# Sending most of a result ahead of its last columns: one store, or two

## The chip, the cores and the metric

The kernel runs on one core of one Trainium2 chip. The metric is the device time of one execution in microseconds; quoted times are medians of several executions. All quoted runs are in the fast state with a granted clock of 1.0.

## The reference

```python
def setup_inputs():
    batch, seq, dim = 32, 512, 1024
    return {"x": np.random.randn(batch, seq, dim).astype(np.float32)}

def reference(x):
    relu_x = np.maximum(x, 0)
    return np.mean(relu_x, axis=-1).astype(np.float32)
```

It reads 67 MB and writes 64 KB: one mean for each of 16384 rows.

## The kernel before

The first 128 rows are handled on their own and stored early (512 bytes). The other 16256 are laid out as 128 partitions of 127 rows, so the results stand in a tile `res` of 128 x 127 floats. SyncE issues all loads on one queue: seven of 16 rows a partition, then pieces of 7, 4, 2 and 1 rows, then the last row of each partition in three pieces of columns. ScalarE and VectorE share the rows, and each writes a sum per row. GpSimd scales columns 0 to 111 once the seven big loads are reduced, columns 112 to 124 later, column 125 later still; VectorE writes column 126 itself, last of all. The cut below is the code of `before`, with comments added and lines left out at each `...`.

```python
    J = J - 1                       # 127 result columns
    NB = 16
    full = J // NB                  # 7 big loads
    j0 = full * NB                  # 112
    ...
    def finish(after, lo, hi):
        nc.gpsimd.wait_ge(act, after)
        nc.gpsimd.wait_ge(dve, after)
        nc.gpsimd.tensor_scalar(
            out=res[:, lo:hi], in0=sums[:, lo:hi], scalar1=inv, scalar2=0.0, op0=ALU.mult, op1=ALU.add,
        )
    ...
    finish(full, 0, j0)
    ...
    finish(i, j0, j0 + lo)
    ...
    nc.vector.wait_ge(loaded[i + 2], 16)                       # the middle column piece
    dve_row(nc, last[:, 512:768], last[:, D + 1:D + 2]).then_inc(dve, 1)
    nc.vector.wait_ge(act, n_done + 1)
    nc.vector.wait_ge(dve, n_done + 1)
    nc.vector.wait_ge(loaded[i + 3], 16)                       # the last column piece
    nc.vector.scalar_tensor_tensor(
        out=last[:, 768:], in0=last[:, 768:], scalar=0.0, in1=scale[:, :], op0=ALU.max, op1=ALU.mult,
        accum_out=res[:, J - 1:J],
    ).then_inc(dve, 1)

    nc.sync.wait_ge(pool, 2)
    nc.sync.wait_ge(dve, n_done + 2)
    nc.sync.dma_start(out=outr, in_=res[:, :]).then_inc(stored, 16)
    nc.sync.sem_clear(...)
    nc.sync.wait_ge(stored, 32).then_inc(stored, -32)
```

## Time and profile before

| | |
|---|---|
| time, median of 3 runs | 161.32 us (161.29 to 161.35) |
| span of the profile | 160.2 us |
| last load packet ends | 157.38 us |
| VectorE's last signal | 158.51 us |
| last landing of the store | 160.21 us |

The last three rows are from the trace's records of packets and of semaphore signals. The trace has 16 closing packets of 4 bytes and 16 semaphore signals for each load and store of the last stretch; a "landing" is such a signal, and the waiting engine goes on after the last of the 16. In this document the *tail* is the time from VectorE's last signal to the end of the span, 1.74 us here. Only the tail is the store's; what comes before it is the stream of loads and the last reductions.

### The profile page before, as it was taken

Reading aid. Unit: us, or ns where it says so; the run is one execution under the profiler, and the core shown is the slowest. Engines: PE = TensorE matmul, PEld = TensorE weight load, DVE = VectorE, ACT = ScalarE, POOL = GpSimd, SP = SyncE. Lnnn points to the kernel's source line nnn. Section 1 sums busy time; section 2 is a strip of 40 time slices with the busy share of each in tenths; the row PEclk is TensorE's granted clock in tenths of the full one; section 3 lists DMA queues with packets and bytes.
Section 4 is the critical chain, followed back from the end, with each engine's and each line's share of the span. In section 5 each row is a group of like instructions: output and inputs, shape, how many; then the busy total and the mean of one; then the engine's idle time right before and its main releaser. Section 6 shows DMA issues by size and latency. Waiting matters only on the chain. (4 is left out here: it accounts for less than half of the span.)

```text
span 160.2 us, 347 instructions
## 1 busy us (share of the span) xinstructions
DVE 73.3 (46%) x131; ACT 70.4 (44%) x133; POOL 1.3 (1%) x9
## 2 busy tenths in 40 slices
DVE  0000029900498006960079500993009920299984
ACT  1400029800496006950079300991009900299983
POOL 1000000000000000000000000000000000000001
DMA  9969969979989899699699699699699797998992
GB/s 393 507 278 523 507 278 523 442 344 523 409 376 523 360 425 524 294 491 523 262 524 523 262 523 524 262 523 523 262 524 458 327 523 327 425 451 367 419 412 102
DMA packets 2312, 67.18 MB, mean 419 GB/s; under 512 B 392, under 2 KB 648, under 8 KB 1032
## 3 DMA queue, kind: packets, MB, share of 16 engines
q1 hardware_dynamic: 2312, 67.18, 97.7%
HBM read 67.11 MB, written 0.07 MB: 419 GB/s over the span
## 5 line engine op out<-in xcount | busy, mean ns | idle before, releaser
L20 DVE TENSOR_SCALAR_CACHE_REDUCE rows<-rows 128x1024 f32<-128x1024 f32 (+1 forms) x63 | 72.1, 1208 | 78.9 <-DMA rows<-in_x_dram 78.7
L15 ACT ACTIVATE rows<-rows 128x1024 f32<-128x1024 f32 x64 | 66.2, 1035 | 84.1 <-DMA rows<-in_x_dram 83.9
L15 ACT ACTIVATION_READ_ACCUMULATOR rows<-rows 128x1 f32 x64 | 11.9, 186 | 0.0
L20 DVE DVE_READ_ACCUMULATOR rows<-rows 128x1 f32 x63 | 5.2, 82 | 0.0
L168 DVE STREAM_TRANSPOSE turned<-mean 128x32 f32<-128x32 f32 x1 | 0.2, 213 | 5.9 <-ACT row L164 5.9
L164 ACT ACT_TABLE_LOAD x1 | 1.3, 1283 | 3.3 <-DMA row<-in_x_dram 3.3
L157 POOL TENSOR_SCALAR res<-sums 128x112 f32<-128x112 f32 (+1 forms) x2 | 0.5, 250 | 154.0 <-DVE rows L20 154.0
L164 ACT ACTIVATE row<-row 128x1024 f32<-128x1024 f32 x1 | 1.1, 1056 | 0.0
L15 ACT ACTIVATE last<-last 128x512 f32<-128x512 f32 x1 | 0.6, 630 | 0.0
L20 DVE TENSOR_SCALAR_CACHE_REDUCE last<-last 128x256 f32<-128x256 f32 x1 | 0.4, 420 | 0.3 <-DMA last<-in_x_dram 0.3
L197 DVE SCALAR_TENSOR_TENSOR last<-last,scale 128x258 f32<-128x258 f32 x1 | 0.4, 428 | 0.1
L142 POOL MEMSET scale<- 128x258 f32 x1 | 0.3, 314 | 0.0
L187 POOL TENSOR_SCALAR res<-part 128x1 f32<-128x1 f32 x1 | 0.3, 267 | 0.6 <-DVE rows L20 0.6
L164 ACT ACTIVATION_READ_ACCUMULATOR row<-row 128x1 f32 x1 | 0.2, 186 | 0.0
L15 ACT ACTIVATION_READ_ACCUMULATOR last<-last 128x1 f32 x1 | 0.2, 186 | 0.0
L141 POOL MEMSET mean<- 128x32 f32 x1 | 0.1, 126 | 1.5 <-POOLq L55 1.5
L232 POOL MEMSET const-uint8-127<- 128x1 uint8 x1 | 0.1, 103 | 0.0
L232 POOL MEMSET const-bfloat16-1.0<- 128x1 bf16 x1 | 0.1, 102 | 0.0
L232 POOL MEMSET const-float32-0.0<- 128x1 f32 x1 | 0.1, 99 | 0.2 <-issue 0.2
L232 POOL MEMSET const-float32-1.0<- 128x1 f32 x1 | 0.1, 99 | 0.0
L20 DVE DVE_READ_ACCUMULATOR last<-last 128x1 f32 x1 | 0.1, 83 | 0.0
L197 DVE DVE_READ_ACCUMULATOR last<-last,scale 128x1 f32 x1 | 0.1, 82 | 0.0
## 6 DMA issues: line engine op xcount, KB each, us to landing
rows<-in_x_dram SPq DMA_DIRECT2D x1, 3584.0 KB, 38.1
rows<-in_x_dram SPq DMA_DIRECT2D x1, 2048.0 KB, 42.6
rows<-in_x_dram SPq DMA_DIRECT2D x1, 1024.0 KB, 44.7
row<-in_x_dram SPq DMA_DIRECT2D x1, 512.0 KB, 3.3
rows<-in_x_dram SPq DMA_DIRECT2D x1, 512.0 KB, 45.4
last<-in_x_dram SPq DMA_DIRECT2D x1, 256.0 KB, 45.6
last<-in_x_dram SPq DMA_DIRECT2D x2, 128.0 KB, 45.4
rows<-in_x_dram SPq DMA_DIRECT2D x7, 48.8
```

The source lines that it names most:

```text
L15: return nc.scalar.activation(out=src, in_=src, func=ACT.Relu, accum_out=acc)
L20: return nc.vector.tensor_scalar(out=src, in0=src, scalar1=0.0, scalar2=init, op0=ALU.max, op1=ALU.add, accum_out=acc,)
L141: nc.gpsimd.memset(mean0[:, :], 0.0)
L142: nc.gpsimd.memset(scale[:, :], inv).then_inc(pool, 1)
L157: nc.gpsimd.tensor_scalar(out=res[:, lo:hi], in0=sums[:, lo:hi], scalar1=inv, scalar2=0.0, op0=ALU.mult, op1=ALU.add,)
L164: nc.scalar.activation(out=row0[:, :], in_=row0[:, :], func=ACT.Relu, scale=inv, accum_out=mean0[:, 0:1],).then_inc(first, 1)
L168: nc.vector.transpose(turned0[:, :], mean0[:, :]).then_inc(first, 1)
L187: nc.gpsimd.tensor_scalar(out=res[:, J - 2:J - 1], in0=part[:, 0:1], scalar1=part[:, 1:2], scalar2=inv, op0=ALU.add, op1=ALU.mult,).then_i ...
L197: nc.vector.scalar_tensor_tensor(out=last[:, 768:], in0=last[:, 768:], scalar=0.0, in1=scale[:, :], op0=ALU.max, op1=ALU.mult, accum_out=r ...
L232: nc = _bacc.Bacc("TRN2", target_bir_lowering=False, num_devices=1)
```

## The change

The intent is to take bytes off the store that stands at the end: 112 of the 127 columns have been ready since about 149 us. They go out in a store of their own, queued behind the loads, and the last store carries 15 columns.

```diff
@@ in finish
             out=res[:, lo:hi], in0=sums[:, lo:hi], scalar1=inv, scalar2=0.0, op0=ALU.mult, op1=ALU.add,
-        )
+        ).then_inc(pool, 1)
@@ at the end
     nc.sync.wait_ge(pool, 2)
+    nc.sync.dma_start(out=outr[:, :j0], in_=res[:, :j0]).then_inc(stored, 16)
     nc.sync.wait_ge(dve, n_done + 2)
-    nc.sync.dma_start(out=outr, in_=res[:, :]).then_inc(stored, 16)
+    nc.sync.wait_ge(pool, 4)
+    nc.sync.dma_start(out=outr[:, j0:], in_=res[:, j0:]).then_inc(stored, 16)
 ...
-    nc.sync.wait_ge(stored, 32).then_inc(stored, -32)
+    nc.sync.wait_ge(stored, 48).then_inc(stored, -48)
```

## The prediction

> **What bounds the kernel now.** I read the page first, for the shares of busy time and the slices, then the waits, then the timeline of the last four microseconds, and last a table of short stretches at the end of the span with the packet records of the trace beside it.
>
> The page says what holds the kernel as a whole:
>
> ```profile
> span 160.2 us, 347 instructions
> DVE 73.3 (46%) x131; ACT 70.4 (44%) x133; POOL 1.3 (1%) x9
> ...
> q1 hardware_dynamic: 2312, 67.18, 97.7%
> HBM read 67.11 MB, written 0.07 MB: 419 GB/s over the span
> ```
>
> The two computing engines are busy less than half of the span, and the packets on the one DMA queue fill 97.7% of it. So the kernel is a stream of 67 MB of loads, with a short head and a short tail around it. The change touches no load; all it can move lies in the tail, between the last load packet (ends at 157.38 us in the packet records) and the end of the span at 160.24 us: 2.86 us, 1.8% of the span.
>
> The waits of the issuing queue say the same from its side (columns: total us, times, longest):
>
> ```profile
> SPq L204 <- DVE last L197: 45.6, 1, 45.6
> SPq L210 <- SPq L210: 1.2, 1, 1.2
> ```
>
> From the end of its last load issue (112.9 us) to the end of the last reduction at 158.5 us the queue does nothing: it waits 45.6 us for VectorE, issues the store, and then waits 1.2 us for the store to land. The page's chain of work that ended last gives 0% to everything: it stops at a branch hint in the tail, so I built the chain from the timeline instead (start, duration):
>
> ```profile
> 157.54 0.42 DVE L20 TENSOR_SCALAR_CACHE_REDUCE last<-last 128x256 f32<-128x256 f32 x1 [0.29 <-DMA last<-in_x_dram]
> 157.70 0.19 ACT L15 ACTIVATION_READ_ACCUMULATOR last<-last 128x1 f32 x1
> 157.89 0.08 DVE L20 DVE_READ_ACCUMULATOR last<-last 128x1 f32 x1
> 158.06 0.43 DVE L197 SCALAR_TENSOR_TENSOR last<-last,scale 128x258 f32<-128x258 f32 x1
> 158.41 0.08 DVE L197 DVE_READ_ACCUMULATOR last<-last,scale 128x1 f32 x1
> 158.57 0.35 SPq L205 DMA_DIRECT2D out_dram<-res  x1
> ```
>
> VectorE was released by the middle column piece at 157.54, ran the two last reductions to 158.49, and the store was issued at 158.57. The stretches from there on (length, busy times of DVE, ACT and POOL, clock, then the DMA share and GB/s):
>
> ```profile
> 158.49:158.57 0.08, 0.01 (x1) 0.00 (x0) 0.00 (x0) 1.00 0.00 0
> 158.57:159.41 0.84, 0.00 (x0) 0.00 (x0) 0.00 (x0) 1.00 0.00 0
> 159.41:159.78 0.37, 0.00 (x0) 0.00 (x0) 0.00 (x0) 1.00 0.61 176
> 159.78:160.24 0.46, 0.00 (x0) 0.00 (x0) 0.00 (x0) 1.00 0.00 0
> ```
>
> So the store's 1.67 us from issue to end are 0.84 us in which no packet moves, 0.37 us of packets, and 0.46 us from the last packet to the last landing. Only the middle one can depend on bytes by anything seen here.
>
> **What the Trainium skill says.** Three places of the page "DMA: Bandwidth & Descriptors" bear on it. The section "Anatomy of one DMA — SWDGE (gpsimd) path" gives a transfer a fixed part of about 2 us, mostly the receipt of the last write, and a part that grows with bytes. It describes another issuing path, but the trace has the same shape: of 1.67 us, 1.30 (0.84 + 0.46) move no data. The section "Queues, rings and completion order" says that on each DMA engine the descriptors of a ring are consumed in ring order; the trace agrees for the loads, whose 16 closing packets for each of the last three pieces come in order. The section "Rules for kernel authors" says of small transfers to coalesce them, since under 64 KB one pays mostly overhead: both parts of the divided store are such transfers (56 KB and 7.5 KB), so by that rule one store is better unless the first part's overhead is hidden. No page speaks of how two waits ahead of one transfer are placed; for that I use the trace.
>
> **The change part by part.**
>
> Removed: one store of 128 rows of 127 floats (508 bytes a row) at the end. In its place at the end is one of 128 rows of 15 floats (60 bytes a row), as many descriptors as before. The duration of one packet in the trace's records, by size: 4 bytes 9 ns, 128 bytes 13, 508 bytes 27, 1024 bytes 46, 2048 bytes 84. This is a line: (46 - 27) / (1024 - 508) = 0.037 ns a byte, and 27 - 508 x 0.037 = 8.2 ns fixed. A 60 byte packet is then an estimated 8.2 + 2.2 = 10.4 ns. Each of 16 engines moves 8 rows: 8 x 27 = 216 ns now, 8 x 10.4 = 83 after, 133 ns less. The engines start staggered: their closing packets start between 159.607 and 159.762, so less 216 ns their first data packets start about 159.39 to 159.55. If the stagger stays, the end moves by the full 0.13 us. If the descriptors are supplied no faster than they are consumed now, the end moves by less; I count 0.11 us. The 0.84 us and the 0.46 us stay.
>
> Added early: one store of 128 rows of 112 floats (448 bytes, an estimated 24.7 ns a packet, 8 x 24.7 = 0.2 us an engine). It waits for GpSimd's first scaling, which runs at 148.68 for 0.29 us, so it is issued at about 149.0 on a queue that otherwise sleeps until 158.5: its 0.35 us of issue cost nothing. Its packets lie behind the loads in the rings, start on each engine when that one's last load is done (closing packets between 156.99 and 157.37), and are over by about 157.6, or 158.1 with a landing of 0.46 us. The final packets do not start before 159.4, so the two stores do not meet, and the last wait (now for 48 instead of 32) is still ended by the second one.
>
> Moved: the waits. Now the store has two waits, written GpSimd first, VectorE second. The trace shows the second as an instruction of its own (the VectorE wait is counted at L204, and 17 ns long) and the first one carried by the transfer itself; the loads with two waits have the same split. From VectorE's signal at 158.507 to the issue at 158.57 are 0.063 us. In the change VectorE's wait is written first, so by the same rule the transfer itself carries it. Instructions that carry the wait that ends last start 17 to 24 ns after the signal in this tail (VectorE's at 157.542 after the landing at 157.518; the final wait at 160.226 after 160.209). So 0.04 us may be saved; since no transfer here shows it, I count 0.03. No instruction is added on the path.
>
> GpSimd's two added signals ride on existing instructions of an engine that is 1% busy: nothing.
>
> Sum: -0.11 - 0.03 = -0.14 us. 161.32 - 0.14 = 161.18 us, 0.09% less.
>
> **The rivals.**
>
> First, nothing moves at the end: the tail is latency and the number of descriptors, which is the same 128. Against it: in the 0.37 us of packets the mean DMA share is 0.61, and the engines' own packets lie one behind the other, so these are bytes being moved. For it: I have seen no 60-byte packet, and rows that start at odd multiples of 4 bytes may cost more on the memory side than the line says. The section "Specifications" of the same page says that below 512 bytes a transfer does read-modify-write; 508 and 60 are both below, and no run shows yet whether it is dearer for 60. Then 161.3.
>
> Second, the early store delays the last loads. Its packets begin on the first engine at 157.0, while the slowest engine still reads its last piece until 157.37. That last piece has landed at 157.82, and VectorE, with its own earlier work, goes on only at 157.98, so there are 0.16 us of slack for it. The middle piece has none (157.518 to 157.542), but its last closing packet started at 156.97, before any packet of the early store can start. So only a delay over 0.16 us would count; 8 packets of 25 ns on an engine that is already done with its loads can hardly make one. If they did, perhaps +0.1 to +0.2: 161.4.
>
> Third, the second transfer is slower to issue or land because the first was issued: it writes the rest of the same rows of memory. The first has landed more than a microsecond before. 161.4 at most.
>
> A fourth, the intent: that the store's whole cost hides behind the loads. It cannot: the last columns are known only at 158.49, and a transfer with 1.30 us of fixed time follows whatever its size. This would make it 159.7 only if the last store vanished.
>
> **Range and chances.** All the rivals lie within -0.3 and +0.25 us of 161.32. Three runs of before lie within 0.06 us, and a different instruction stream may shift a run by some 0.1. So 161.18 us, with 160.95 to 161.40 eight times in ten. Two per cent is 3.2 us, more than the whole tail of 2.86, so faster by over 2% is impossible but for a side effect on the loads, and slower by that much would need the loads disturbed for microseconds: 0.01 each, 0.98 within 2%.
>
> **What would show it.** Each step has its place in the profile of the changed kernel. The early store's issue stands at about 149.0. Its 128 packets of 448 bytes stand between 157.0 and 157.6, and VectorE's two last reductions still end near 158.5. The gap from the end of the last reduction to the store's issue shrinks from 0.08 to about 0.04. The stretch with packets of 60 bytes is about 0.24 us long instead of 0.37, and those ahead and behind stay at 0.84 and 0.46. It would be wrong if the packets of 60 bytes last nearer 27 ns than 10, if the stretch after the last packet grows, or if the last reductions start later than 158.06 because the last column piece lands later.

## The result, and the profile after

| | before | after |
|---|---|---|
| median of 6 runs each, same rounds | 161.40 us (161.29 to 161.78) | 161.19 us (161.07 to 161.81) |
| ratio | | 0.9989, 95% interval 0.9971 to 1.0008 |

A ratio is the mean time of one kernel's fast runs over the mean of the other's in the same rounds, so it is not quite the ratio of the medians. The clock alone cannot even tell the sign for sure, since single executions of one kernel differ by up to 0.7 us here. The trace can: from profile to profile the pieces of the tail that should not change differ by 23 ns at most (one landing of 444 ns, where the others are near 400, is looked into below).

The page of the changed kernel (the total, and the one queue: packets, MB, share):

```profile
span 159.8 us, 348 instructions
...
q1 hardware_dynamic: 2456, 67.18, 97.9%
```

One instruction more, the second transfer, and 144 packets more, its 128 rows and 16 closing packets. The bytes are the same.

The waits of the issuing queue after (total us, times, longest):

```profile
SPq L205 <- POOL res L157: 35.9, 1, 35.9
SPq L207 <- POOL res L187: 8.3, 1, 8.3
SPq L213 <- SPq L213: 1.0, 1, 1.0
SPq L208 <- DVE last L197: 0.7, 1, 0.7
```

The one wait of 45.6 us is now three: until GpSimd has scaled 112 columns, then until it has done the rest, then 0.7 us for VectorE. The final wait for the landing is 1.0 us instead of 1.2. Note that VectorE's wait is now counted at L208, the line of the transfer itself, where before it had a line of its own.

The timeline of the queue and of VectorE's last instructions after (start, duration):

```profile
148.81 0.35 SPq L205 DMA_DIRECT2D out_dram<-res  x1
...
157.84 0.43 DVE L197 SCALAR_TENSOR_TENSOR last<-last,scale 128x258 f32<-128x258 f32 x1
158.19 0.08 DVE L197 DVE_READ_ACCUMULATOR last<-last,scale 128x1 f32 x1
158.30 0.34 SPq L208 DMA_DIRECT2D out_dram<-res  x1
```

and the stretches of the tail after (length, busy times, clock, DMA share, GB/s):

```profile
158.27:158.30 0.03, 0.01 (x1) 0.00 (x0) 0.00 (x0) 1.00 0.00 0
158.30:159.14 0.84, 0.00 (x0) 0.00 (x0) 0.00 (x0) 1.00 0.00 0
159.14:159.36 0.22, 0.00 (x0) 0.00 (x0) 0.00 (x0) 1.00 0.42 35
159.36:159.78 0.42, 0.00 (x0) 0.00 (x0) 0.00 (x0) 1.00 0.00 0
```

Compared with the four stretches of before in the prediction: the stretch between the last reduction and the issue shrank from 0.08 to 0.03, the wait for the first packet stayed 0.84, the packets take 0.22 instead of 0.37, and the stretch after them is 0.42 instead of 0.46.

The span fell by 0.46 us, more than twice what the clock shows. Only 0.24 of it is the tail (1.736 to 1.496 us). The other 0.22 us was there before the tail began: the last load packet ended at 157.13 instead of 157.38. The packets of the second load, issued at 0.45 us in both, started at 2.52 instead of 2.75, so the stream had that difference from its start. Nothing of the change lies there, and the repeats below show that it is chance.

### The profile page after: what moved, and what is told of

Same layout as the page of the kernel before. It is cut to its first block, busy times and chain, and to the rows that moved or that the text cites. A ratio compares the mean times of both kernels' runs of the same rounds, so it can differ in the third digit from the quotient of the medians.

```text
span 159.8 us, 348 instructions
## 1 busy us (share of the span) xinstructions
DVE 73.3 (46%) x131; ACT 70.4 (44%) x133; POOL 1.3 (1%) x9
```

## The experiments

The theory: the change gains in two places of the tail and nowhere else. The last store's packets are shorter (60 bytes in place of 508), about 0.14 us, and the transfer itself now carries VectorE's wait, about 0.05 us. Rivals: the gain is one of these alone; it needs the large store to be hidden behind the loads; it is the 0.22 us by which the loads ended earlier; the larger landing (0.44 and 0.40) belongs to the kernel before.

This table, worked out from the packet and signal records of each profile, is what the experiments are read by. All in ns. "Gap" is from VectorE's last signal to the start of the issue that follows; "first" from that issue to the first packet of the last store; "packets" from the first packet's start to the last one's end, with the median of one packet in brackets; "landing" from there to the last landing. A further 33 or 34 to the end of the span complete the tail. (The kernel with two stores at the end doesn't fit the columns and is told below.)

| kernel | row bytes of the last store | gap | first | packets (one) | landing | tail |
|---|---|---|---|---|---|---|
| before | 508 | 63 | 848 | 347 (27) | 444 | 1736 |
| before, again | 508 | 63 | 843 | 354 (27) | 396 | 1690 |
| order of the waits only | 508 | 17 | 843 | 349 (27) | 391 | 1634 |
| after | 60 | 16 | 838 | 207 (11) | 402 | 1496 |
| after, again | 60 | 16 | 840 | 207 (11) | 402 | 1498 |
| after, old order of waits | 60 | 63 | 839 | 208 (11) | 393 | 1536 |
| large store late | 60 | 17 | 840 | 203 (11) | 397 | 1490 |
| cut in half | 252 | 16 | 844 | 260 (18) | 390 | 1543 |
| three stores | 8 | 17 | 827 | 193 (9) | 384 | 1454 |
| eight early stores | 60 | 17 | 829 | 203 (11) | 780 | 1863 |
| eight early stores, again | 60 | 17 | 825 | 207 (11) | 792 | 1875 |
| eight early stores by rows | 60 | 16 | 846 | 207 (11) | 400 | 1503 |
| small rows in one early store | 60 | 16 | 842 | 209 (11) | 1914 | 3014 |

The times of the experiments, in three groups that each shared a chip and its runs of before:

| kernel | median us | before, same rounds | ratio, 95% interval |
|---|---|---|---|
| order of the waits only | 161.41 | 161.37 | 1.0003 (0.9986 to 1.0020) |
| after, old order of waits | 161.18 | 161.37 | 0.9979 (0.9966 to 0.9993) |
| large store late | 161.12 | 161.37 | 0.9979 (0.9965 to 0.9993) |
| after, again | 161.13 | 161.37 | 0.9978 (0.9964 to 0.9993) |
| cut in half | 161.33 | 161.42 | 1.0000 (0.9984 to 1.0015) |
| eight early stores | 161.39 | 161.42 | 0.9990 (0.9978 to 1.0002) |
| two at the end | 161.76 | 161.42 | 1.0024 (1.0010 to 1.0039) |
| before, again | 161.34 | 161.42 | 0.9999 (0.9987 to 1.0012) |
| small rows in one early store | 163.13 | 161.39 | 1.0110 (1.0091 to 1.0128) |
| eight early stores by rows | 161.32 | 161.39 | 1.0000 (0.9981 to 1.0020) |
| three stores | 161.17 | 161.39 | 0.9988 (0.9969 to 1.0007) |
| eight early stores, again | 161.85 | 161.39 | 1.0022 (1.0009 to 1.0035) |

All results were correct but the one that is wrong.

### The order of the waits alone

The kernel before, with two lines changing places:

```diff
-    nc.sync.wait_ge(pool, 2)
     nc.sync.wait_ge(dve, n_done + 2)
+    nc.sync.wait_ge(pool, 2)
     nc.sync.dma_start(out=outr, in_=res[:, :]).then_inc(stored, 16)
```

> One store as in the kernel before; only its two waits change places, VectorE's first. Tail means the time from VectorE's last signal to the end of the span: 1.74 us in the profile of before, 1.50 in that of the change. Theory (two gains in the tail: the order of the waits, and the shorter packets): the gap from that signal to the store's issue falls from 0.063 to about 0.016 us, the packets stay 27 ns and last 0.35 us in all, the tail is 1.69, the time 0.05 us less than before (not to be told from it by the clock alone). Rival (the order of the waits has nothing to do with it, the short gap came from the wait for GpSimd that was over early): the gap stays 0.06.

The gap fell from 63 to 17 ns, and the packets stayed at 27 ns and 0.35 us. The stretches from the issue on:

```profile
158.24:159.09 0.85, 0.00 (x0) 0.00 (x0) 0.00 (x0) 1.00 0.00 1
159.09:159.44 0.35, 0.00 (x0) 0.00 (x0) 0.00 (x0) 1.00 0.64 185
159.44:159.86 0.42, 0.00 (x0) 0.00 (x0) 0.00 (x0) 1.00 0.00 0
```

The theory's gap is right. The tail is 1.63 and not the expected 1.69, because the landing took 391 ns instead of 444; that was not expected of this experiment. The clock shows no gain (161.41 against 161.37); one of 0.05 us is too small for it.

### The change with the old order of the waits

```diff
-    nc.sync.wait_ge(dve, n_done + 2)
     nc.sync.wait_ge(pool, 4)
+    nc.sync.wait_ge(dve, n_done + 2)
     nc.sync.dma_start(out=outr[:, j0:], in_=res[:, j0:]).then_inc(stored, 16)
```

> The change, but with the two waits of the last store in the old order (GpSimd's first). Theory: gap 0.063 us as before, packets of 60 bytes at 11 ns, 0.21 us in all, tail 1.50 + 0.05 = 1.55; time about 0.15 to 0.2 us under before. Rival (all of the gain is the waits): the packets are short but the tail is 1.7.

```profile
158.71:158.79 0.08, 0.00 (x1) 0.00 (x0) 0.00 (x0) 1.00 0.00 0
158.79:159.62 0.83, 0.00 (x0) 0.00 (x0) 0.00 (x0) 1.00 0.00 0
159.62:159.84 0.22, 0.00 (x0) 0.00 (x0) 0.00 (x0) 1.00 0.42 35
```

The gap is back at 63 ns and the packets are as short as in the change: 1.536 us of tail. With the run above, the two gains are separate and add up: 46 or 47 ns for the waits, 139 to 147 ns for the packets. This profile is of the longest of its five executions (161.60 us), in which the loads ended late, at 157.59; its tail was no longer for that.

### The large store issued late

```diff
-    nc.sync.wait_ge(pool, 2)
+    nc.sync.wait_ge(pool, 4)
     nc.sync.dma_start(out=outr[:, :j0], in_=res[:, :j0]).then_inc(stored, 16)
```

> The change, but the large store is issued only when GpSimd has done everything, at about 157.5 us instead of 148.8, so it is not queued behind the loads and moves at about 158.4, with the DMA engines idle before it. Theory (what counts is only that the bytes left the last store, wherever they went before it): the last store's issue, packets and landing as in the change, tail 1.50, time as the change's. Rival (the gain needs the large store hidden behind the loads): the last store's first packet or landing comes later, by up to 0.3 us, and the time is that of before or more.

```profile
157.47 0.35 SPq L205 DMA_DIRECT2D out_dram<-res  x1
...
158.26 0.34 SPq L208 DMA_DIRECT2D out_dram<-res  x1
```

```profile
158.31:158.66 0.35, 0.00 (x0) 0.00 (x0) 0.00 (x0) 1.00 0.59 164
158.66:159.10 0.44, 0.00 (x0) 0.00 (x0) 0.00 (x0) 1.00 0.00 0
159.10:159.32 0.22, 0.00 (x0) 0.00 (x0) 0.00 (x0) 1.00 0.42 35
159.32:159.73 0.41, 0.00 (x0) 0.00 (x0) 0.00 (x0) 1.00 0.00 0
```

The first stretch is now the large store, alone on the DMA engines and 0.44 us ahead of the small one. The tail is 1.490, that of the change, and so is the time. The place behind the loads is worth nothing by itself; it was enough that the large store was issued 0.78 us before VectorE's last signal (157.47 and 158.25). A later issue was not tried, but for both stores at the end, below.

### The change again, and the kernel before again

> The change once more, for a second profile. Theory: tail 1.50 within 0.05, wherever the loads end; the end of the load packets may move by 0.2 us either way between profiles. Rival (the difference of the two spans, 0.46 us, is all the work of the change): the load packets end at 157.13 again and the span is 159.8 again within 0.05.

> The kernel before once more, for a second profile. Theory: gap 0.063, packets of 27 ns in 0.35 us, and the landing after the last packet about 0.40, as in the four other new profiles, since the 0.444 of the first profile was chance: tail 1.69. Rival (the old kernel's landing is longer by 0.04 by its nature): 0.44 again, tail 1.74.

The second profile of the change has the same tail to 2 ns (1.498). Its span is 159.842, within the 0.05 us that the rival allowed, and its loads ended at 157.15, so this run alone does not refute that rival. The second profile of before does: its loads ended at 157.14, where they end in the changed kernel, and its span is 159.99 us, not 160.24.

```profile
158.29:158.36 0.07, 0.00 (x0) 0.00 (x0) 0.00 (x0) 1.00 0.00 0
158.36:159.20 0.84, 0.00 (x0) 0.00 (x0) 0.00 (x0) 1.00 0.00 0
159.20:159.57 0.37, 0.00 (x0) 0.00 (x0) 0.00 (x0) 1.00 0.61 176
159.57:159.98 0.41, 0.00 (x0) 0.00 (x0) 0.00 (x0) 1.00 0.00 0
```

So the first profile of before had a late stream of loads and a long landing (444 against 396), both by chance. (Its execution took 161.59 us, where the three timed runs took 161.29 to 161.35.) Between like profiles the change is worth 1.690 - 1.496 = 0.194 us.

### Another cut

```diff
-    nc.sync.dma_start(out=outr[:, :j0], in_=res[:, :j0]).then_inc(stored, 16)
+    nc.sync.dma_start(out=outr[:, :64], in_=res[:, :64]).then_inc(stored, 16)
 ...
-    nc.sync.dma_start(out=outr[:, j0:], in_=res[:, j0:]).then_inc(stored, 16)
+    nc.sync.dma_start(out=outr[:, 64:], in_=res[:, 64:]).then_inc(stored, 16)
```

> The change cut at another column: 64 columns go out early, the last 63 (252 bytes a row) at the end. Theory (the last store's packets cost 8.2 ns plus 0.037 ns a byte, eight to an engine one after the other): packets of 17.5 ns, the stretch of packets 0.347 - 8 x (27 - 17.5) / 1000 = 0.27 us, tail 1.49 + 0.06 = 1.55 to 1.56. Rival (a step, not a line: any row under some size is as cheap as 60 bytes, or any row is as dear as 508 but for very small ones): 11 ns and 0.21 us, or 27 ns and 0.35 us.

```profile
159.31:159.59 0.28, 0.00 (x0) 0.00 (x0) 0.00 (x0) 1.00 0.54 115
```

18 ns a packet, 0.26 us of packets, tail 1.543: the line holds at this size too, and neither step of the rival is there. The times, 161.33 against 161.42, are too close to add to that.

### Two stores at the end

```diff
-    nc.sync.wait_ge(pool, 2)
-    nc.sync.dma_start(out=outr[:, :j0], in_=res[:, :j0]).then_inc(stored, 16)
     nc.sync.wait_ge(dve, n_done + 2)
     nc.sync.wait_ge(pool, 4)
     nc.sync.dma_start(out=outr[:, j0:], in_=res[:, j0:]).then_inc(stored, 16)
+    nc.sync.dma_start(out=outr[:, :j0], in_=res[:, :j0]).then_inc(stored, 16)
```

> Both stores at the end, the 15 columns first and the 112 columns right behind them, none early. Theory (the fixed time of a store hides only where nothing waits for it; at the end each further transfer costs its issue): second issue some 0.39 us after the first and 0.44 long, first of its packets 0.5 us after that, packets 0.32, landing 0.40: tail 2.05 to 2.10, time 0.35 us over before. Rival (issuing is cheap beside moving, two transfers in a row overlap wholly): tail 1.65 to 1.75, time that of before.

```profile
158.34 0.35 SPq L206 DMA_DIRECT2D out_dram<-res  x1
158.73 0.43 SPq L207 DMA_DIRECT2D out_dram<-res  x1
```

The second issue starts 0.39 us after the first, its first packet comes at 159.66, and the tail is 2.09 us: a second transfer costs 0.4 us where something waits for it. The time is 0.34 us over before in the medians, and clear of it. The same two transfers are 0.19 us better or 0.4 us worse in the tail than one, by when the first of them is issued.

### Eight early stores

```diff
-    nc.sync.dma_start(out=outr[:, :j0], in_=res[:, :j0]).then_inc(stored, 16)
+    for k in range(0, j0, 14):
+        nc.sync.dma_start(out=outr[:, k:k + 14], in_=res[:, k:k + 14]).then_inc(stored, 16)
 ...
-    nc.sync.wait_ge(stored, 48).then_inc(stored, -48)
+    nc.sync.wait_ge(stored, 160).then_inc(stored, -160)
```

> The change, but the early 112 columns go out in eight stores of 14 columns instead of one, all queued behind the loads: 1024 packets of about 10 ns, some 0.7 us on each engine instead of 0.2, with eight times the closing packets. Theory (behind the loads in the rings they can't delay a load, and they are done before 159): the last column piece lands 0.44 to 0.49 us after the last load packet, as in all five profiles so far, VectorE's last signal comes 1.13 to 1.20 us after it, tail 1.50, time as the change's. Rival (stores on engines that are done with their loads slow the others' last piece or its landing): the landing takes 0.6 us or more, and the time rises by 0.15 us or more.

This went against the theory. The last packets of the early stores ended at 157.65, well before 159, but:

```profile
158.35:159.18 0.83, 0.00 (x0) 0.00 (x0) 0.00 (x0) 1.00 0.00 0
159.18:159.40 0.22, 0.00 (x0) 0.00 (x0) 0.00 (x0) 1.00 0.42 35
159.40:160.20 0.80, 0.00 (x0) 0.00 (x0) 0.00 (x0) 1.00 0.00 0
```

The last store's packets are unchanged and its landing takes twice as long, 780 ns, which neither the theory nor the rival had foreseen. The landing of the last column piece of the loads also rose, from 475 ns after the last load packet to 614, as the rival had it; VectorE's slack took that up (its last signal came 1.18 us after the last load packet, in the theory's range). The clock shows no loss against before (161.39 and 161.42). The run's six times fell between 161.08 and 161.54, and the profile is of one of the longest, so the experiment was repeated:

> The eight early stores of 14 columns once more, since its six runs fell into two groups (161.08 to 161.25 and 161.54) and its profile was of the slow group. If the long landing is there in every execution: last landing 0.6 to 0.8 again and a median near 161.4. If it is a chance of some executions: a profile with a landing of 0.40 goes with a time near 161.1.

The landing was 792 ns this time, and all six times lay between 161.63 and 162.02, with a median of 161.85 where 161.4 was expected. The loads' last landing came even later, 729 ns after the last load packet, and this was more than VectorE's slack: its last signal came 1.30 us after that packet. The two profiled executions differ by 0.47 us: the loads ended 0.34 us later, VectorE's signal came another 0.11 us later, and the tails differ by 0.01. The tail's loss is there in both profiles, but both are of longer executions of their runs (161.54 and 162.01), so it is not shown for those of 161.08 to 161.25. Why the six executions of the first run were on average 0.5 us faster is not explained.

### Which property of the eight stores does it

Two more kernels take apart what the eight stores have more of: small rows, and closing packets. The first is wrong (every 14th of the early columns isn't written), so as to have the small rows in a single transfer:

```diff
-    nc.sync.dma_start(out=outr[:, :j0], in_=res[:, :j0]).then_inc(stored, 16)
+    gaps = lambda ap: ap.rearrange("p (a b) -> p a b", b=14)[:, :, :13]
+    nc.sync.dma_start(out=gaps(outr[:, :j0]), in_=gaps(res[:, :j0])).then_inc(stored, 16)
```

> Wrong result on purpose: the early columns go out in one store again, but as eight pieces of 13 columns a row with one column left out after each, so 1024 packets of 52 bytes with only 16 closing packets (the eight-store run had 1024 packets of 56 bytes with 128 closing packets; its early landings trailed from 157.4 to 159.3 us, though its packets ended at 157.65, and its last landing took 0.78 us in place of 0.40). Theory A (many small writes to memory are received more slowly than their packets run): the same trail, early landings until 159, the last store's landing 0.6 to 0.8 us, tail 1.7 to 1.9. Theory B (it is the number of closing packets): early landings done by 158.3, last landing 0.40, tail 1.50.

The second has eight transfers with the change's 128 packets of 448 bytes:

```diff
-    nc.sync.dma_start(out=outr[:, :j0], in_=res[:, :j0]).then_inc(stored, 16)
+    for p in range(0, P, 16):
+        nc.sync.dma_start(out=outr[p:p + 16, :j0], in_=res[p:p + 16, :j0]).then_inc(stored, 16)
 ...
-    nc.sync.wait_ge(stored, 48).then_inc(stored, -48)
+    nc.sync.wait_ge(stored, 160).then_inc(stored, -160)
```

> Eight early stores again, but cut by rows: 16 rows of 112 columns each, so 128 packets of 448 bytes as in the change, with 128 closing packets in place of 16. Theory A (small writes): early landings done by 158.1, last landing 0.40, tail 1.50, as in the change. Theory B (closing packets): the trail and the long last landing as with eight stores of 14 columns, tail 1.7 to 1.9.

The last stretch of each, from the last packet to the end; first the small rows in one store, then the eight stores by rows:

```profile
159.73:161.66 1.93, 0.00 (x0) 0.00 (x0) 0.00 (x0) 1.00 0.00 0
```

```profile
159.52:159.94 0.42, 0.00 (x0) 0.00 (x0) 0.00 (x0) 1.00 0.00 0
```

The long last landing goes with the 1024 small rows and not with the closing packets: 1914 ns with 16 closing packets, 400 ns with 128. The eight stores by columns and those by rows show the same with 128 closing packets and the same bytes in both: 780 and 792 ns with 1024 rows of 56 bytes, 400 ns with 128 rows of 448. The number of the rows and their size change together here. The first kernel was slower than before by 1.7 us, and its tail of 3.01 us is far over the 1.7 to 1.9 that theory A allowed. Signals of landings of its two stores came in from 158.4 to 161.6 us, mixed.

Theory A has a miss too. With the eight stores by rows, the early landings should have been done by 158.1; they came from 157.48 to 159.25, 128 of them, (159.25 - 157.48) / 127 = 0.014 us apart. That trail is the closing packets', as theory B had it, and it ended before the last store's own landings began (159.71), so it cost the last store nothing. So the trail and the long last landing, which had looked like one thing, are two. These stores also delayed the last loads' landing, to 607 ns after the last load packet, and their time was that of before (161.32 against 161.39), so the change's gain is not seen there by the clock.

It is not simply that the early stores were still landing. In the first run with eight stores by columns, 128 signals had come by 159.34 us, all that the early stores give (the next, 159.58, fits the first of the last store, as in the other profiles); that is before the last store's packets ended at 159.38, and its landing was long all the same. In the repeat and with the small rows in one store, signals of the early stores were still outstanding at that point.

What stays open: why many small pieces make the last landing long, by what path, whether it is their number or their size (128 early rows of 52 bytes did no harm in the three stores below: 384 ns), and why pieces that lie side by side in one transfer (1914 ns) are worse than the same number spread over eight (780 and 792). The pieces of the two kernels differ in order, in size (52 and 56 bytes) and in their gaps, and these runs do not separate that.

### Three stores

```diff
     nc.sync.dma_start(out=outr[:, :j0], in_=res[:, :j0]).then_inc(stored, 16)
+    nc.sync.wait_ge(pool, 3)
+    nc.sync.dma_start(out=outr[:, j0:J - 2], in_=res[:, j0:J - 2]).then_inc(stored, 16)
 ...
-    nc.sync.dma_start(out=outr[:, j0:], in_=res[:, j0:]).then_inc(stored, 16)
+    nc.sync.dma_start(out=outr[:, J - 2:], in_=res[:, J - 2:]).then_inc(stored, 16)
 ...
-    nc.sync.wait_ge(stored, 48).then_inc(stored, -48)
+    nc.sync.wait_ge(stored, 64).then_inc(stored, -64)
```

> The change driven one step on, the one version left that could beat it: 112 columns early, 13 columns at about 156.6 us when GpSimd has scaled them, and only the last two (8 bytes a row) at the end. Packet line: 8.2 + 0.3 = 8.5 ns, eight of them 68 ns against 83: stretch of packets 0.19 us instead of 0.207, tail 1.48, time as the change's to within 0.02. If theory A is right in a strong form (256 early packets, half of them small, are too many already), the last landing is over 0.45 and the time is worse than the change's.

9 ns a packet and 193 ns of packets, as worked out. The tail is 1.454 us, 42 ns under the change's, of which 14 are the packets and the rest lies in "first" (827) and "landing" (384), which a single profile can't tell from chance. By the clock it is the change's equal (161.17 us). It is not shown to beat it.

## Why the prediction was right

The range (160.95 to 161.40) held the measured 161.19, and the middle (161.18) was nearly exact. That it was so exact is luck: the gain was counted as 0.14 us where the tail shows 0.19, and it was taken from 161.32, the median of three runs, where six runs of before gave 161.40 in the rounds of the change. The two errors nearly cancel (161.40 - 0.19 = 161.21). By its steps:

- *The tail is all that can move, and the time stays within 2%.* Right: 0.194 us between like profiles, and a ratio of 0.9989 with an interval that contains 1. Later rounds put the same kernel at 0.9978, with an interval below 1.
- *The packets of 60 bytes.* The line gave 10.4 ns, measured 11; it also gave 17.5 at 252 bytes (measured 18) and 8.5 at 8 bytes (measured 9). The prediction then cut the 0.133 us it had worked out to 0.11, in case the rows are supplied too slowly. They are not: 0.140 to 0.147 us was gained. The cut was unneeded.
- *The order of the waits.* The rule read off the loads held: the wait that is written first is carried by the transfer. 0.03 us was counted; 0.047 was measured, and confirmed in both directions.
- *The 0.84 us stay.* 825 to 848 ns in every profile of the table, whatever the rows' size and whatever went before.
- *The 0.46 us stay.* They do. 0.42 after and 0.46 before looked like a gain, and the second profile of before showed 0.41. Taken at face value, the first pair of profiles would have credited the change with 0.24 us.
- *The early store does not delay the last loads.* Right for the change: the last column piece landed 475 and 490 ns after the last load packet, against 444 and 474 in the two profiles of before, inside VectorE's slack. But one argument for it was wrong. The early packets were to stand between 157.0 and 157.6, with the loads ending at 157.38, and so behind every packet of the middle column piece, which has no slack. They stood between 156.59 and 157.30, with the loads ending at 157.13, so the first began 0.53 us before the last load packet ended, not 0.38. The last engine's 8 packets of 46 ns for the last piece leave its middle piece to end near 156.75 (an estimate: 157.125 - 8 x 0.046 - 0.009), after the first early packets. The middle piece landed no later for that: 174 ns after the last load packet, and 173 in the second profile of before. Nor is it right of early stores in general: with eight of them the last piece landed after 607 to 729 ns, and with the small rows after 806; at 729 and 806 VectorE's last signal was late as well (1.30 and 1.38 us after the last load packet, against 1.13 to 1.20 in before and after).
- *The last store is not slowed by the early one.* The reason given was that the early one has landed more than a microsecond before. It had, by 157.84 us. With small rows in one early store it had not, and there the last landing did become longer. But this reason is not shown to be the one that counts: the large store issued late landed only by 159.03, 0.08 us before the last store's first packet, and the last landing was 397 ns; the eight early stores by columns had landed by 159.34, and it was 780.

The sum of -0.14 us was thus too small by 0.05 us, on both terms in the cautious direction; the true number is near -0.19.

## What to carry to other kernels

The last store of a kernel is paid in a fixed part, here about 1.29 us of the changed kernel's tail (16 + 838 + 402 + 33 ns), and a part that goes with its bytes, here 8.2 ns plus 0.037 ns a byte for each of eight rows on an engine; taking bytes off it gains only the second, and costs nothing if the one transfer that takes them is issued while nothing waits. Keep that early transfer in few long rows: cut into 1024 rows of some 50 bytes it went with a final landing of 0.8 to 1.9 us instead of 0.40, though the packets themselves looked as short as ever; why is not shown. And take a second profile of the kernel before, before crediting a change with a few hundredths of the tail.

## What the Trainium skill lacked or had wrong

- "DMA: Bandwidth & Descriptors", section "Specifications", has one threshold, 512 bytes, below which a transfer does read-modify-write. All last stores here are below it, and rows of 508, 252, 60 and 8 bytes, 128 of them, landed 384 to 402 ns after their last packet (444 once). With 1024 rows of 52 or 56 bytes in earlier stores, whose packets had ended 1.5 to 1.8 us before the last store's first, the landing was 780 to 1914 ns. The page gives no figure for what small rows of an earlier store do to the landing of a later one.
- The same page, section "Rules for kernel authors", says to coalesce small transfers. At the end of the kernel that held (a second transfer cost 0.4 us). Two transfers of 56 and 7.5 KB nonetheless beat one of 63.5 KB by 0.19 us in the tail, since the first one's fixed part lay where nothing waited. The row on coalescing does not say so, but the section is not silent: its row on overlap has the fixed setup cost of a transfer overlap when it is issued early, and the runs agree (tail 1.50 us with the first store issued early, 2.09 with both at the end).
- The same page, section "Anatomy of one DMA — SWDGE (gpsimd) path", calls the semaphore write essentially free. With 128 closing packets on one semaphore the landings came 14 ns apart for 1.77 us, the last of them 1.8 us after the last of these packets. The runs do not tell whether the semaphore writes took that time or what each had to wait for, so the page is not shown to be wrong.
- No page says which of two waits the transfer carries itself. ("Perfetto Trace Analysis", section "Identifying Dependency Chains", says only that further waits may stand in instructions of their own ahead of it, so the prediction's word that no page speaks of it was too wide.) Here it is the one written first, and having the last-ending wait there saves 46 to 47 ns.
